# Twelve load slots for the small experts, and four accumulators for the last scatter

## The chip, the cores and the metric

The kernel runs on one core of a Trainium2 chip. The metric is the device time of one execution in microseconds (us). Most executions of a kernel here agree within 0.3%. A core has a matmul engine (TensorE, PE in the rows; its weight loads are PEld), a vector engine (VectorE, DVE), an activation engine (ScalarE, ACT), GpSimd (POOL) and SyncE (SP), which here issues the loads. Sixteen DMA engines move data from the chip's memory (HBM) into the on-chip memory (SBUF); matmuls accumulate in PSUM.

## The reference

A two-layer backbone over 256 latent tokens and 256 context tokens, width 1024: attention of three kinds, then a dense SwiGLU in layer 0 and a top-2-of-8 mixture of experts in layer 1, then a last RMSNorm. All in float32. The part that the change touches is the mixture and the norm behind it:

```python
def swiglu(h, wg, wu, wd):
    return (jax.nn.silu(h @ wg) * (h @ wu)) @ wd

def moe_swiglu(h, w_router, wg, wu, wd):
    t = h.reshape(-1, shp[-1])
    logits = (t @ w_router).astype(jnp.float32)
    top_v, top_i = lax.top_k(logits, TOP_K)
    top_w = jax.nn.softmax(top_v, axis=-1)
    gates = jnp.sum(jax.nn.one_hot(top_i, N_EXPERTS, dtype=jnp.float32) * top_w[..., None], axis=1)
    for e in range(N_EXPERTS):
        y = y + gates[:, e:e + 1].astype(t.dtype) * swiglu(t, wg[e], wu[e], wd[e])
...
        x = x + ga2[:, None] * ffn(h_lat)
...
    return rmsnorm(x, g_final)
```

Each expert has three matrices of 1024 x 3584 (wg, wu) and 3584 x 1024 (wd), 44 MB in float32, and all eight are read.

## The kernel before

The kernel works through layer 0, the attention of layer 1 and then, from about 1080 us on, the experts. Expert 0 comes first, the others in the order of how many tokens chose them. The first four (NBIG) get a block of 128 gathered tokens each and are called full here; the last four get 64 tokens and are called small.

A full expert (`expert`, L1184) reads weight blocks of 1 MB with `load_e` (L1076). Each block is converted on chip to a pair of float32r tiles, eh and el (`convert`, L788: ScalarE at L804, VectorE at L805), and TensorE multiplies with the pair in three passes (`mm3`). The converted tiles have buffers of their own: two of each kind in the pool `mpr` and one of each in `mpc`; loads take them in the order `(mpr, mpr, mpc)[i % 3]` (L1079), so the last two loads of the last full expert, number 174 and 175, have the two of `mpr`.

A small expert (`expert_small`, L1235) has half the rows and multiplies the loaded float32 block directly, with no conversion (`load_raw`, L1226). It goes through the 3584 hidden columns in four rounds j of 896. In a round come four times a gate and an up load of 256 x 896 (0.92 MB each) and their matmuls into `pgs` (L1274), then SiLU and product (L1284, L1285); the transposes (L1246) and the down step of the round before (`down_s`, L1251) come in the round after, with three loads of 256 x 1024 (1.05 MB), one of 128 x 1024 (0.52 MB) and matmuls into `pds` (L1261). So a round has twelve loads and 11.0 MB. The last down step of an expert, and the scatter of its result into the tokens (`t1`, L1298), run inside the first round of the expert after it.

Every load takes the next name of a list, the ring (`slot32`, L1066), takes its buffer, and puts the name back at the end. The ring begins with ten names; five of them leave at given load numbers (`until`, L914), and from load 62 on there are five: w, c, r0, r1, r2, of 1 MB each. The buffer is free when the instruction that last read it is done: VectorE's conversion for a load of a full expert, TensorE's last matmul on it for one of a small expert. The loads stand in one order on SyncE's queue, and a load that waits holds up all behind it. Besides that each load waits for the landing of the one eight before it, since eight semaphores (DMAHW0 to 7 in the order) tell of landings in turn.

The scatter (L1313 to L1322) scales the expert's 64 rows (VectorE, into the tile shown as xT), spreads them over the 256 tokens with four matmuls, two column halves o for each token half t, into `py`, one of two PSUM banks of the pool `pmt`, and adds each to the tokens `xtk` on VectorE. After the last expert `square` (L1337) does, for each column half, ScalarE's sum of squares and VectorE's product with the norm's gain into `xg`; `finish` (L1343) adds the sums, takes the root and scales and stores the output.

Of the kernel before, what the change touches and what calls it, by code (L numbers as in the profile page):

```python
# [11 lines left out]
F32 = mybir.dt.float32  # L12
# [3 lines left out]
AF = mybir.ActivationFunctionType  # L16
ALU = mybir.AluOpType
# [3 lines left out]
P = 128  # L21
# [6 lines left out]
NE = 8  # L28
# [4 lines left out]
NBIG = 4  # L33
# [58 lines left out]
def hybrid_backbone_kernel(  # L92
# [6 lines left out]
    act = nc.scalar.activation  # L99
    tt = nc.vector.tensor_tensor  # L100
# [33 lines left out]
    def bank(pool, name):  # L134
        return pool.tile([P, 512], F32, tag="b", name=name)
# [754 lines left out]
    for k in range(KD):  # L890
        t = tmp("nt2")[:, :NL]
# [4 lines left out]
    mp = pool("mp")  # L896
# [7 lines left out]

    slots = {"w": lambda: mpw.tile([P, 2048], F32, tag="w32", name="e32"),
             "c": lambda: mpc.tile([P, 2048], F32, tag="w32", name="e32"),
             "xh": lambda: mp.tile([P, 2048], F32, tag="xeH0", name="e32"),
             "xl": lambda: mp.tile([P, 2048], F32, tag="xeL0", name="e32"),
             "xt": lambda: mp2.tile([P, 2048], F32, tag="xtk", name="e32"),
# [85 lines left out]
    def part(ap, o):  # L995
        return ap[:, 2 * o:2 * o + 2]

    def half(ap):
        return ap.rearrange("p (a n) -> p a n", n=NL)
# [235 lines left out]
    def expert_small(xs, wg, wu, wd, e, tail, hooks, end=None):  # L1235
        H = P // 2
        xv = xs[:, :, (e - NBIG) * H:(e - NBIG + 1) * H]
        pd = [None]

        HB = FB // 2  # L1240
        NB = FE // FB

        def g_Ts(g):
            pt = bank(pmt, "pgt")
            for q in range(FK):
                nc.tensor.transpose(pt[:, q * H:(q + 1) * H], g[0:H, q * P:(q + 1) * P], ident[0:H, 0:H])  # L1246
            gt = mp2.tile([P, FK, H], F32, tag="gts", name="gts")
            copy_bal(gt, pt[:, 0:FK * H].rearrange("p (q n) -> p q n", n=H))
            return gt

        def down_s(gt, j):  # L1251
            if pd[0] is None:
                pd[0] = pdn.tile([P, 512], F32, tag=f"pd{e % 2}", name="pds")
            for q0 in range(0, FK, 2):
                kn = min(2, FK - q0)
                r0 = j * FB + q0 * P
                w = load_raw(wd[r0:r0 + kn * P, :].rearrange("(k p) n -> p k n", p=P), kn, D)
                for k in range(kn):
                    q = q0 + k
                    for o in range(2):  # L1260
                        mm(pd[0][H * o:H * o + H, :], lhsT=gt[:, q, :], rhs=w[:, k, o * 512:(o + 1) * 512],  # L1261
                           start=j == 0 and q == 0, stop=j == NB - 1 and q == FK - 1, skip_group_check=True)

        prev = None
        for j in range(NB):
            ps = pgu.tile([P, 2, 512], F32, tag=("pg", "pu")[j % 2], name="pgs")
            for c in range(KD // 2):
                ws = [load_raw(w_ap[c * 256:(c + 1) * 256, j * FB:(j + 1) * FB].rearrange("(k p) n -> p k n", p=P), 2, FB)
                      for w_ap in (wg, wu)]
                for k in range(2):  # L1270
                    kk = 2 * c + k
                    for b in range(2):
                        for o in range(2):
                            mm(ps[H * o:H * o + H, b, 0:HB], lhsT=xv[:, kk, :], rhs=ws[o][:, k, b * HB:(b + 1) * HB],  # L1274
                               start=kk == 0, stop=kk == KD - 1, skip_group_check=True)
                if c == 1:
                    if prev is not None:
                        gt = g_Ts(prev)
                    elif tail:
                        tail[0]()  # L1280
            g = mp2.tile([P, FB], F32, tag="es", name="es")
            for b in range(2):
                gv = g[0:H, b * HB:(b + 1) * HB]
                act(gv, ps[0:H, b, 0:HB], AF.Silu)  # L1284
                tt(gv, gv, ps[H:P, b, 0:HB], ALU.mult)  # L1285
            if prev is not None:
                down_s(gt, j - 1)
            elif tail:
                tail[1]()
            prev = g  # L1290
            for f in (hooks or {}).get(j, ()):
                f()
        last = []

        def t0():
            last.append(g_Ts(prev))

        def t1():  # L1298
            if end:
                tc.keep_in_program_order(nc.scalar.preload_act_table_set(LN_EXP))  # L1300
                new_xg()
            down_s(last[0], NB - 1)
            pt = bank(pmt, "pst")
            for t in range(2):
                nc.tensor.transpose(pt[:, t * P:(t + 1) * P], f32(S[:, t, e, :]), ident)
            for t in range(2):
                mm(pt[:, 256:257], lhsT=f32(S[:, t, e, :]), rhs=gatp[:, t, e:e + 1], start=t == 0, stop=t == 1)
            ST = mp2.tile([P, 256], F32, tag="ST", name="STs", bufs=2)
            nc.vector.tensor_copy(ST, pt[:, 0:256])
            gs = mp.tile([P, 1], F32, tag="gs", name="gs", bufs=2)  # L1310
            nc.vector.tensor_copy(gs, pt[:, 256:257])
            yo = part(y32, e % 2)
            stt(yo, half(pd[0]), gs, ga2s, op0=ALU.mult, op1=ALU.mult)  # L1313
            for t in range(2):
                pys = []
                for o in range(2):
                    py = bank(pmt, "py")
                    mm(py, lhsT=ST[H * o:H * o + H, t * P:(t + 1) * P], rhs=yo[H * o:H * o + H], start=True, stop=True)
                    pys.append(py)
                for o in range(2):  # L1320
                    cs = slice(o * 512, (o + 1) * 512)
                    tt(xtk[:, t, cs], xtk[:, t, cs], pys[o], ALU.add)  # L1322
            if end:
                for o in range(2):
                    end(o)
        return t0, t1

    xg = None
# [5 lines left out]
    ssq4 = mp.tile([P, 2, 2], F32, name="ssq4")  # L1334
    junk = xT[:, 4:6, 0:NL]

    def square(o):  # L1337
        for t in range(2):
            xo = half(xtk[:, t, o * 512:(o + 1) * 512])
            act(junk, xo, AF.Square, accum_out=ssq4[:, t, o:o + 1])  # L1340
            tt(half(xg[:, t, o * 512:(o + 1) * 512]), xo, part(gfb, o), ALU.mult)

    def finish():  # L1343
        tt(ssq, ssq4[:, :, 0], ssq4[:, :, 1], ALU.add)
# [15 lines left out]
    xes = {}  # L1360
# [21 lines left out]
    for e in range(NE):  # L1382
        if e == 0:
            ws = [w[0, 0] for w in (wm_g, wm_u, wm_d)]
        else:
            ws = [w[0, ds(which[e], 1)].rearrange("o a b -> (o a) b") for w in (wm_g, wm_u, wm_d)]
        hooks = {j: f for (ee, j), f in plan.items() if ee == e}
        if e >= NBIG:
            tail = expert_small(xes[NBIG], *ws, e, tail, hooks, square if e == NE - 1 else None)
            continue  # L1390
        xe, h = (x01, e * P) if e < 2 else (xes[2], (e - 2) * P)
        xv = (xe[0][:, :, h:h + P], xe[1][:, :, h:h + P])
        gt_ = gates if e == 0 else gatp
        tail = expert(xv, *ws, lambda t, e=e: S[:, t, e, :], lambda t, e=e, g=gt_: g[:, t, e:e + 1], tail, hooks, e == 0)
    tail[0]()
    tail[1]()
    finish()

    cv = nc.values_load(cnti[0:1, 0:1], min_val=0, max_val=NL)
    with tc.If(cv > 0):  # L1400
        pc = mp3.tile([P, 2], F32, name="pc")
        gc = mp3.tile([P, 2], F32, name="gc")
        bc = mp3.tile([P, 1], F32, name="bc")
        S2 = mp3.tile([P, 2, P], F32R, name="S2")
        xe2 = xe_tiles(1)
        for blk in range(2):
            with tc.For_i(0, NE, 1) as ei:
                nc.vector.tensor_copy(pc, posm[:, :, ds(ei, 1)].rearrange("p t o -> p (t o)"))
                nc.vector.tensor_copy(gc, gates[:, :, ds(ei, 1)].rearrange("p t o -> p (t o)"))
                nc.vector.tensor_copy(bc, base[:, ds(ei, 1)])  # L1410
                ts_(pc, pc, bc, float(P * blk), op0=ALU.subtract, op1=ALU.subtract)
                for t in range(2):
                    ts_(S2[:, t, :], tb("iota", tab2, TAB_C), pc[:, t:t + 1], None, op0=ALU.is_equal)
                gather(lambda t: S2[:, t, :], P, xe2)
                xv = (xe2[0][:, :, 0:P], xe2[1][:, :, 0:P])
                sq_ = lambda w: w[0, ds(ei, 1)].rearrange("o a b -> (o a) b")
                for f in expert(xv, sq_(wm_g), sq_(wm_u), sq_(wm_d), lambda t: S2[:, t, :], lambda t: gc[:, t:t + 1], None):
                    f()
        new_xg()
        for o in range(2):  # L1420
            square(o)
        finish()


# [29 lines left out]
```

## Time and profile before

| | |
|---|---|
| median of 3 runs | 1977.64 us (1975.27 to 1979.37) |
| profiled execution | 1976.52 us, of it 1974.7 us between the first and the last instruction (the span) |
| TensorE busy in the span | 1816.8 us (92%) |
| VectorE, ScalarE busy | 979.2 us, 758.7 us |
| read from HBM | 477.39 MB |

Times in rows are microseconds from the span's start, unless marked ns. The share of the DMA engines is the time that packets took over sixteen engines' time; it can be a little over 1 where packets overlap. A wait in the rows is put down to what ended it. The small experts run from about 1500 us to the end.

### The profile page before, as it was taken

The numbers are of one execution on the slowest core, as the hardware profiler recorded it, in microseconds if no ns is written. First come the engines' busy times: TensorE is split into PE (matmuls) and PEld (weight loads), VectorE is DVE, ScalarE is ACT, GpSimd is POOL, SyncE is SP. The second block draws the span as 40 slices with busy tenths as digits, with TensorE's granted clock in tenths as the row PEclk, the third lists the DMA queues.
The fourth block names the chain that finished last, engine by engine and source line by source line (L and its number), as shares of the span: only waits on it lengthen the run. The fifth ranks groups of instructions, "written<-read, shape, count | busy, mean of one in ns | idle before, by whom it ended". The sixth has DMA issues, their size and how long they took to land.

```text
span 1974.7 us, 23529 instructions
## 1 busy us (share of the span) xinstructions
PE 1816.8 (92%) x9280; PEld 1259.1 (64%) x9280; DVE 979.2 (50%) x1294; ACT 758.7 (38%) x965; POOL 46.7 (2%) x75
## 2 busy tenths in 40 slices
PE   7998999999999999999899999999998878887876
PEld 4756766778877887777687878888785322222222
DVE  5474555633333345755678888988984101010101
ACT  3424454422222224345566777777662000000001
POOL 1030000000000000210000000000000000000000
PEclk8999999999999999999989999999999999999998
DMA  8765243342334334553489789999998999999996
GB/s 281 223 178 143 70 132 100 115 144 70 101 99 156 110 108 155 158 140 128 146 298 360 255 305 330 334 356 361 353 340 317 366 388 388 388 382 402 396 397 249
DMA packets 261922, 480.05 MB, mean 243 GB/s; under 512 B 11630, under 2 KB 141996, under 8 KB 261804
## 3 DMA queue, kind: packets, MB, share of 16 engines
q1 hardware_dynamic: 259296, 474.19, 67.8%
q0 software_dynamic: 1312, 2.62, 0.9%
q10 hardware_dynamic: 1196, 1.66, 0.3%
q8 instruction: 75, 1.23, 0.3%
q14 instruction: 43, 0.35, 0.1%
HBM read 477.39 MB, written 1.05 MB: 242 GB/s over the span
## 4 chain that ended last, share of the span: by engine, by line
PE 74%; DMA 15%; DVE 7%; ACT 3%; issue 2%; SPq 0%; POOL 0%; DVEq 0%; ACTq 0%; POOLq 0%
DMA e<-in_w_moe_up_dram 10%; PE pd L1146 8%; PE pgs L1274 6%; DMA e<-in_w_moe_down_dram 3%; PE pu L152 3%; PE pg L151 3%; PE pu L153 3%; PE pg L152 3%; PE pu L151 3%; PE pg L153 2%; PE pds L1261 2%; PE psg L151 2%; PE psu L151 2%; PE psu L152 2%; PE psu L153 2%; PE psd L151 2%
## 5 line engine op out<-in xcount | busy, mean ns | idle before, releaser
L805 DVE TENSOR_TENSOR el<-e,eh 128x2048 fp32r<-128x2048 f32 (+1 forms) x173 | 375.4, 2189 | 49.5 <-ACT eh L804 48.8
L804 ACT ACTIVATE eh<-e 128x2048 fp32r<-128x2048 f32 (+1 forms) x173 | 316.7, 1839 | 93.1 <-PE pu L153 32.7
L1274 PE MATMUL pgs<-e,xs 128*64 128x448 f32 x1024 | 228.7, 557 | 71.1 <-DMA e<-in_w_moe_up_dram 64.4
L1274 PEld LDWEIGHTS pgs<-e,xs 128*64 128x64 f32 x1024 | 75.6, 138 | 218.7 <-DMA e<-in_w_moe_up_dram 105.0
L144 ACT ACTIVATE wh<-w 128x2048 fp32r<-128x2048 f32 (+2 forms) x70 | 125.4, 1791 | 208.4 <-issue 80.0
L145 DVE TENSOR_TENSOR wl<-w,wh 128x2048 fp32r<-128x2048 f32 (+2 forms) x70 | 149.6, 2138 | 97.9 <-ACT wh L144 97.9
L1285 DVE TENSOR_TENSOR es<-es,pgs 64x448 f32<-64x448 f32 x32 | 19.9, 623 | 324.0 <-ACT es L1284 324.0
L1284 ACT ACTIVATE es<-pgs 64x448 f32<-64x448 f32 x32 | 17.2, 537 | 325.6 <-PE pgs L1274 315.2
L1261 PE MATMUL pds<-e,gts 128*64 128x512 f32 x448 | 109.6, 599 | 9.9 <-DMA e<-in_w_moe_down_dram 9.0
L151 PE MATMUL pg<-eh,xeH 128*128 128x512 f32 x224 | 89.7, 400 | 0.6 <-ACT eh L804 0.6
L151 PE MATMUL psp<-hH,wh 128*128 128x512 f32 (+1 forms) x224 | 86.7, 391 | 3.1 <-ACT hH L276 3.0
L152 PE MATMUL pg<-el,xeH 128*128 128x512 f32 x224 | 89.4, 399 | 0.0
L151 PE MATMUL pu<-eh,xeH 128*128 128x512 f32 x224 | 88.8, 397 | 0.0
L152 PE MATMUL pu<-el,xeH 128*128 128x512 f32 x224 | 88.2, 394 | 0.7 <-DVE el L805 0.6
L151 PE MATMUL psq<-wh,hH 128*128 128x256 f32 x304 | 88.5, 291 | 0.0
L153 PE MATMUL pg<-eh,xeL 128*128 128x512 f32 x224 | 88.5, 395 | 0.0
L152 PE MATMUL psq<-wl,hH 128*128 128x256 f32 x304 | 87.7, 289 | 0.0
L153 PE MATMUL pu<-eh,xeL 128*128 128x512 f32 x224 | 87.7, 391 | 0.0
L153 PE MATMUL psq<-wh,hL 128*128 128x256 f32 x304 | 87.4, 287 | 0.0
L152 PE MATMUL psp<-hL,wh 128*128 128x512 f32 (+1 forms) x224 | 86.1, 384 | 0.0
L153 PE MATMUL psp<-hH,wl 128*128 128x512 f32 (+1 forms) x224 | 85.6, 383 | 0.0
L1261 PEld LDWEIGHTS pds<-e,gts 128*64 128x64 f32 x448 | 32.0, 136 | 68.6 <-issue 39.0
(504 smaller groups left out, 3470.8 us busy)
## 6 DMA issues: line engine op xcount, KB each, us to landing
e<-in_w_moe_down_dram SPq DMA_DIRECT2D x103, 1024.0 KB, 7.9
e<-in_w_moe_gate_dram SPq DMA_DIRECT2D x64, 896.0 KB, 7.8
e<-in_w_moe_up_dram SPq DMA_DIRECT2D x64, 896.0 KB, 7.1
e<-in_w_moe_gate_dram SPq DMA_DIRECT2D x55, 1024.0 KB, 7.3
e<-in_w_moe_up_dram SPq DMA_DIRECT2D x55, 1024.0 KB, 6.5
wmod<-in_w_mod_dram SPq DMA_DIRECT2D x96, 512.0 KB, 5.7
w<-in_w_in_dram SPq DMA_DIRECT2D x24, 1024.0 KB, 8.0
w<-in_w_ffn_gate_dram SPq DMA_DIRECT2D x11, 1024.0 KB, 5.8
```

Source lines behind the costliest of these rows:

```text
L144: act(wh[:, :m], w32[:, :m], AF.Copy)
L145: tt(wl[:, :m], w32[:, :m], f32(wh[:, :m]), ALU.subtract)
L151: mm(ps, lhsT=sh, rhs=mh, start=first, stop=False)
L152: mm(ps, lhsT=sh, rhs=ml, start=False, stop=False)
L153: mm(ps, lhsT=sl, rhs=mh, start=False, stop=last)
L804: act(h3[:, b], w[:, b], AF.Copy)
L805: tt(l3[:, b], w[:, b], f32(h3[:, b]), ALU.subtract)
L1146: mm(pds[o], lhsT=gt[sh][:, q, :], rhs=w[mh][:, k, o * 512:(o + 1) * 512], start=a and j == 0 and q == 0, stop=z and j == NJ - 1 and q == 3)
L1261: mm(pd[0][H * o:H * o + H, :], lhsT=gt[:, q, :], rhs=w[:, k, o * 512:(o + 1) * 512], start=j == 0 and q == 0, stop=j == NB - 1 and q == F ...
L1274: mm(ps[H * o:H * o + H, b, 0:HB], lhsT=xv[:, kk, :], rhs=ws[o][:, k, b * HB:(b + 1) * HB], start=kk == 0, stop=kk == KD - 1, skip_group_c ...
L1284: act(gv, ps[0:H, b, 0:HB], AF.Silu)
L1285: tt(gv, gv, ps[H:P, b, 0:HB], ALU.mult)
```

## The change

The ring gets seven names more when the first small expert begins its second round: the two pairs of `mpr` (mh, ml, twice), the pair of `mpc` (ch, cl) and a tile of the first gather (xm). These were in use by the full experts alone. Names at the front are used first, so the first five loads of that round have the old slots, and the sixth is the first with a new one. The names are taken off again ahead of the branch for experts with too many tokens, which does not run on these inputs.

The last scatter writes its four results into the two double banks of the gate and up accumulators, which are free by then, in place of two banks in turn; its four additions are kept in order, and squares and products follow them all.

```diff
     slots = {"w": lambda: mpw.tile([P, 2048], F32, tag="w32", name="e32"),
              "c": lambda: mpc.tile([P, 2048], F32, tag="w32", name="e32"),
+             "mh": lambda: mpr.tile([P, 2048], F32, tag="wh", name="e32"),
+             "ml": lambda: mpr.tile([P, 2048], F32, tag="wl", name="e32"),
+             "ch": lambda: mpc.tile([P, 2048], F32, tag="wh", name="e32"),
+             "cl": lambda: mpc.tile([P, 2048], F32, tag="wl", name="e32"),
+             "xm": lambda: mp.tile([P, 2048], F32, tag="xeL1", name="e32"),
...
         for j in range(NB):
+            if e == NBIG and j == 1:
+                ring.extend(["mh", "ml", "mh", "ml", "ch", "cl", "xm"])
...
+            keep = tc.keep_in_program_order if end else lambda i: i
+            pys = {}
+            if end:
+                spare = [pgu.tile([P, 2, 512], F32, tag=tag, name="py") for tag in ("pg", "pu")]
             for t in range(2):
-                pys = []
                 for o in range(2):
-                    py = bank(pmt, "py")
+                    py = spare[o][:, t] if end else bank(pmt, "py")
                     mm(py, lhsT=ST[H * o:H * o + H, t * P:(t + 1) * P], rhs=yo[H * o:H * o + H], start=True, stop=True)
-                    pys.append(py)
+                    pys[t, o] = py
                 for o in range(2):
                     cs = slice(o * 512, (o + 1) * 512)
-                    tt(xtk[:, t, cs], xtk[:, t, cs], pys[o], ALU.add)
+                    keep(tt(xtk[:, t, cs], xtk[:, t, cs], pys[t, o], ALU.add))
             if end:
-                for o in range(2):
-                    end(o)
+                end()
...
-    def square(o):
+    def squares():
         for t in range(2):
-            xo = half(xtk[:, t, o * 512:(o + 1) * 512])
-            act(junk, xo, AF.Square, accum_out=ssq4[:, t, o:o + 1])
-            tt(half(xg[:, t, o * 512:(o + 1) * 512]), xo, part(gfb, o), ALU.mult)
+            for o in range(2):
+                act(junk, half(xtk[:, t, o * 512:(o + 1) * 512]), AF.Square, accum_out=ssq4[:, t, o:o + 1])
+        for t in range(2):
+            for o in range(2):
+                cs = slice(o * 512, (o + 1) * 512)
+                tc.keep_in_program_order(tt(half(xg[:, t, cs]), half(xtk[:, t, cs]), part(gfb, o), ALU.mult))
...
+    ring[:] = [nm for nm in ring if nm in ("w", "c", "r0", "r1", "r2")]
```

The order of SyncE's loads is the same before and after; what they wait for is not. The rows are the loads of the second round of the first small expert, from its fifth on, and the first of the third round, before the change (other instructions of the queue stand between them). PE_49 is a wait for TensorE, DVE_49 for VectorE, DMAHW0_49 to DMAHW7_49 one for the load eight back.

```order
L1232 DMA e32_11841<-in_w_moe_gate_dram 128x2x896 [waits DMAHW4_49,DVE_49]
L1232 DMA e32_11843<-in_w_moe_up_dram 128x2x896 [waits DMAHW5_49,PE_49]
L1232 DMA e32_11853<-in_w_moe_gate_dram 128x2x896 [waits DMAHW6_49,PE_49]
L1232 DMA e32_11855<-in_w_moe_up_dram 128x2x896 [waits DMAHW7_49,PE_49]
L1232 DMA e32_11871<-in_w_moe_down_dram 128x2x1024 [waits DMAHW0_49,PE_49]
L1232 DMA e32_11877<-in_w_moe_down_dram 128x2x1024 [waits DMAHW1_49,PE_49]
L1232 DMA e32_11883<-in_w_moe_down_dram 128x2x1024 [waits DMAHW2_49,PE_49]
L1232 DMA e32_11889<-in_w_moe_down_dram 128x1024 [waits DMAHW3_49,PE_49]
L1232 DMA e32_11894<-in_w_moe_gate_dram 128x2x896 [waits DMAHW4_49,PE_49]
```

The same loads after the change:

```order
L1237 DMA e32_11841<-in_w_moe_gate_dram 128x2x896 [waits DMAHW4_49,DVE_49]
L1237 DMA e32_11843<-in_w_moe_up_dram 128x2x896 [waits DMASW4_49,DMASW3_49,DMASW5_49,DMASW2_49,DMASW6_49,DMASW1_49,DMASW7_49,DMASW0_49,PE_49]
L1237 DMA e32_11853<-in_w_moe_gate_dram 128x2x896
L1237 DMA e32_11855<-in_w_moe_up_dram 128x2x896 [waits PE_49]
L1237 DMA e32_11871<-in_w_moe_down_dram 128x2x1024 [waits DMAHW5_49]
L1237 DMA e32_11877<-in_w_moe_down_dram 128x2x1024 [waits DMAHW6_49]
L1237 DMA e32_11883<-in_w_moe_down_dram 128x2x1024 [waits DMAHW7_49]
L1237 DMA e32_11889<-in_w_moe_down_dram 128x1024 [waits DMAHW0_49]
L1237 DMA e32_11894<-in_w_moe_gate_dram 128x2x896 [waits DMAHW1_49,PE_49]
```

Before, e32_11843 waits for TensorE's last matmul on e32_11807, the first load of its own round. After, it waits for the last full expert's matmuls on eh_11739, the converted load 174, and e32_11855 for those on eh_11757, load 175; the four down loads have no wait for TensorE, and e32_11894, the thirteenth load of the longer ring, is the one that waits for the matmuls on e32_11807. The DMASW names are loads of GpSimd that landed in layer 1's attention.

On VectorE the end of the program stood like this before, from the last scaling (xT) to the scaling of the output:

```order
L1313 SCALAR_TENSOR_TENSOR xT<-pds,gs,xT 128x2x256
L1322 TENSOR_TENSOR xtk<-xtk,py 128x512
L1341 TENSOR_TENSOR xg<-xtk,xT 128x512
L1322 TENSOR_TENSOR xtk<-xtk,py 128x512 x2
L1341 TENSOR_TENSOR xg<-xtk,xT 128x512
L1322 TENSOR_TENSOR xtk<-xtk,py 128x512
L1341 TENSOR_TENSOR xg<-xtk,xT 128x512 x2
L1344 TENSOR_TENSOR ssq<-ssq_7907 128x2
L1354 TENSOR_SCALAR xg<-xg,ssq 128x512 x2
```

It stands like this after:

```order
L1320 SCALAR_TENSOR_TENSOR xT<-pds,gs,xT 128x2x256
L1332 TENSOR_TENSOR xtk<-xtk,py 128x512 x4
L1353 TENSOR_TENSOR xg<-xtk,xT 128x512 x4
L1356 TENSOR_TENSOR ssq<-ssq_7907 128x2
L1366 TENSOR_SCALAR xg<-xg,ssq 128x512 x2
```

The four additions (xtk) are now ahead of the four products (xg); the sum of the squares (ssq) is behind all eight in both. TensorE's order is the same in both.

## Rows read from the trace of the kernel before

**Rows 1.** The chain that ended last, by line, from 1540 to 1956 us.
```profile
by line: DMA e<-in_w_moe_up_dram 44.4%; PE pgs L1274 23.7%; DMA e<-in_w_moe_down_dram 15.9%; PE pds L1261 9.2%; PE py L1318 2.1%; DVE es L1285 1.2%; ACT es L1284 1.1%; PE pgt L1246 0.7%; issue 0.7%; DVE xT L1313 0.5%; PE pbc L1063 0.5%; DVE
```
**Rows 2.** Busy times by stretch; the first row names the columns.
```profile
core 0: us, PE busy (x) PEld busy (x) DVE busy (x) ACT busy (x) POOL busy (x), PEclk, DMA share, GB/s
1525.00:1540.00 15.00, 15.00 (x64) 6.58 (x65) 5.33 (x8) 1.80 (x3) 0.00 (x0) 1.00 0.49 176
1690.00:1720.00 30.00, 24.94 (x111) 9.45 (x111) 1.59 (x4) 1.62 (x3) 0.00 (x0) 0.89 0.99 380
1765.00:1825.00 60.00, 45.11 (x214) 15.38 (x214) 3.12 (x5) 2.69 (x5) 0.00 (x0) 1.00 1.03 406
1810.00:1840.00 30.00, 22.79 (x113) 8.35 (x113) 2.36 (x5) 1.07 (x2) 0.00 (x0) 1.00 1.02 400
1540.00:1955.00 415.00, 327.99 (x1530) 114.96 (x1526) 36.29 (x62) 21.81 (x39) 0.00 (x0) 0.99 1.01 391
```
**Rows 3.** TensorE's waits, 1540 to 1955 us: us in total, times, longest us.
```profile
PE pgs L1274 <- DMA e<-in_w_moe_up_dram: 61.7, 48, 2.7
PE pds L1261 <- DMA e<-in_w_moe_down_dram: 8.4, 15, 2.2
PE pgs L1274 <- DMA e<-in_w_moe_gate_dram: 5.2, 8, 0.8
```
**Rows 4.** Waits of SyncE's queue, 1509 to 1540 us.
```profile
SPq L1232 <- PE pgs L1274: 17.7, 3, 10.0
```
**Rows 5.** Waits of SyncE's queue, 1540 to 1956 us.
```profile
SPq L1232 <- PE pgs L1274: 212.2, 74, 7.2
SPq L1232 <- PE pds L1261: 82.2, 59, 3.3
```
**Rows 6.** SyncE's queue in order of time: start us, us.
```profile
1522.64 0.37 SPq L1232 DMA_DIRECT2D e<-in_w_moe_gate_dram  x1
1533.24 0.37 SPq L1232 DMA_DIRECT2D e<-in_w_moe_up_dram  x1
```
**Rows 7.** DMA, 1525 to 1537 us, in 40 slices of 0.3 us.
```profile
DMA  9999960000000000000000000000001971799999
GB/s 418 418 430 406 406 251 24 36 24 0 0 0 0 0 0 0 0 0 0 0 0 0 0 0 0 0 0 0 0 0 48 191 96 72 299 394 442 418 449 394
```
**Rows 8.** TensorE in order of time, 1517 to 1529 us: start us, us.
```profile
1523.51 1.04 PE L1146 MATMUL pd<-eh,gtl 128*128 128x512 f32 x2
...
1527.81 0.63 PE L1146 MATMUL pd<-eh,gtl 128*128 128x512 f32 x2
```
**Rows 9.** DMA, 1527 to 1956 us: packets, MB, share; then issues, KB each, us to landing.
```profile
q1 hardware_dynamic: 46635, 164.23, 98.7%
q8 instruction: 13, 0.21, 0.2%
q14 instruction: 6, 0.05, 0.0%
...
e<-in_w_moe_gate_dram SPq DMA_DIRECT2D x57, 896.0 KB, 7.9
```
**Rows 10.** DMA, 1948 to 1960 us, in 40 slices of 0.3 us.
```profile
GB/s 396 451 369 382 410 410 410 396 410 423 382 410 410 423 437 410 410 396 396 396 410 369 300 232 205 150 109 68 0 0 0 0 0 0 0 0 0 0 0 0
```
**Rows 11.** VectorE in order of time, 1956 to 1968 us: start us, us.
```profile
1960.59 0.69 DVE L1322 TENSOR_TENSOR xtk<-xtk,py 128x512 f32<-128x512 f32 x1 [1.22 <-PE py L1318]
...
1964.42 1.28 DVE L1341 TENSOR_TENSOR xg<-xtk,xT 128x512 f32<-128x512 f32 x2
1965.62 0.15 DVE L1344 TENSOR_TENSOR ssq<-ssq 128x2 f32<-128x2 f32 x1
```
**Rows 12.** ScalarE in order of time, 1960 to 1968 us: start us, us.
```profile
1965.33 0.18 ACT L1340 ACTIVATION_READ_ACCUMULATOR xT<-xtk 128x1 f32 x1
```
**Rows 13.** TensorE's weight loads, waits from 1540 to 1956 us.
```profile
PEld pgs L1274 <- issue: 80.8, 327, 0.8
PEld pds L1261 <- issue: 38.2, 135, 1.3
```

More of the change, by code (lines that the diff above doesn't have):

```diff
@@ L1388, in hybrid_backbone_kernel @@
         if e >= NBIG:
-            tail = expert_small(xes[NBIG], *ws, e, tail, hooks, square if e == NE - 1 else None)
+            tail = expert_small(xes[NBIG], *ws, e, tail, hooks, squares if e == NE - 1 else None)
             continue
@@ L1419, in hybrid_backbone_kernel @@
         new_xg()
-        for o in range(2):
-            square(o)
+        squares()
         finish()
```

## The prediction

> **What bounds the kernel now.** I read the chain that ended last first, for the stretch of the small experts (1540 to 1956 us): weight loads make 60% of it, 44.4% gate and up loads and 15.9% down loads, TensorE's small matmuls 33% [rows 1]. Then the busy times by stretch: from 1540 to 1955 us the DMA engines are filled (share 1.01) at 391 GB/s, while TensorE is busy 328 of 415 us [rows 2]. So the stage is a stream of weights. TensorE waits 75 us in it for landings (61.7 + 8.4 + 5.2) [rows 3], and has 87 us to spare.
>
> Then I asked whether the stream runs at what it can. It does not: between 1765 and 1825 us it holds 406 GB/s for 60 us, in other 30 us it falls to 380 and, right at the start of the stage (1525 to 1540 us), to 176 with a share of 0.49 [rows 2]. What holds it back is seen on SyncE's queue: its next load waits for TensorE to release a slot, 17.7 us in three waits at the start, the longest 10.0 us [rows 4], and 212 + 82 us in 133 waits after that [rows 5]. Those waits are harmless while older loads are still in flight, and cost where the queue runs dry. The reader is to see one hole in full: the load issued at 1522.64 us is followed by the next only at 1533.24 us [rows 6]; the rate is 251 GB/s in the slice that begins at 1526.5 us, nothing at all moves from 1527.7 us, and it is back at 394 GB/s from 1535.5 us [rows 7].
>
> **The ring, part by part.** The loads, their order and their bytes are unchanged; only what each waits for is. Load 6 after the extension (e32_11843) waited for the first load of its own round (five slots back), which TensorE could use only after finishing the last full expert. Now it takes the older of the two converted buffers that this expert's last down step read. TensorE's last matmul pair on it starts at 1523.51 us and takes 1.04 [rows 8], so the release is at 1524.6 us, not at 1533.2. The next load waits for nothing, the one after for the second buffer, whose last pair starts at 1527.81 and takes 0.63 us: 1528.4 us [rows 8]. Four down loads follow with no wait on TensorE at all. The first wait on a consumer in the new order is that of load 13, for the same release at 1533.2 us that load 6 had; by then seven loads, 6.42 MB or 15.8 us at 406 GB/s, have been queued. The hole is closed.
>
> From 1527 us to the end of the stage 164.23 MB come through queue q1 [rows 9]; by sizes that is all loads from number 6 on (57 gate, 58 up, 64 down). Before, they end in a taper, 300 GB/s in the slice at 1954.6 us to 68 in the one at 1956.1, that is at 1956.4 us [rows 10]. The taper costs 1.0 us against a full rate (0.3 us x (6 x 406 - 1064) / 406) and I keep it.
>
> With no hole, the 164.23 MB start where the earlier loads end, 1526.8 us. What is their rate? The trace gives two ends. Highest for a sustained stretch: 406 (the 60 us row), 404.5 us. Lowest: 391, today's mean with all its dips, 420.0 us. A stretch with an expert switch in it and few dips is at 400 (1810 to 1840 us) [rows 2], 410.6 us. I take 403, between 406 and 400, since deeper slots should remove the dips, while the switches themselves I can't exclude: 407.5 us. The end is 1526.8 + 407.5 + 1.0 = 1935.3 us, 21.1 us ahead of 1956.4. About 8 us of it is the hole, 13 us the dips.
>
> Twelve slots aren't twelve loads in flight: each load also waits for the landing of the one eight before it, by the eight DMA semaphores in the order. Eight loads are some 7.3 MB, 18 us of stream; the longest gap that the ring of five showed was 10.0 us [rows 4], so eight cover it. TensorE does not become the limit: its 328 us of work [rows 2] stand against 407 us of stream. It enters some 13 us of loads behind, and gains about 5 us per 27 us of loads (11.0 MB at 403 GB/s, 79% busy), so it has caught up within 70 us, and the end is again landing, last down step, tail. Slots cost no conversion and no copy; they were free since the full experts' last reads.
>
> A page of the Trainium skill speaks against this: "DMA: Bandwidth & Descriptors", section "Where 436 GB/s comes from", holds that loads from HBM are bound by a share of about 358 GB/s per core. By that figure the 164.23 MB would need 459 us, no depth would help, and the saving would be nothing. The trace disagrees: it already moves 391 GB/s over 415 us and 406 over 60 [rows 2].
>
> **The tail, part by part.** Four PSUM accumulators replace two, so that the second token half's matmuls no longer wait for VectorE's additions, and VectorE's eight operations stand as four additions, then four products. Before, VectorE has no idle time there: from the first addition at 1960.59 to the sum of squares at 1965.62 us eight operations run in 5.03 us, 0.63 each, pairs without a wait in 1.28 [rows 11]. The eight stay, and the sum still stands behind them. Bounds: eight at 0.60, the pitch in such a pair (1.28 less the 0.69 of one single is 0.59, rounded up), make 4.8, eight at 0.69 make 5.5; so -0.2 to +0.5 us. I take -0.1, as dependent neighbours are now further apart. ScalarE's squares, which ended 0.1 us before the sum (1965.33 + 0.18) [rows 12], get their inputs earlier and end ahead of VectorE's products; that wait goes, and the products are what is late. TensorE's second pair ends about as the second addition does.
>
> **Sum.** 21.1 + 0.1 = 21.2 us off the profiled execution, 1976.52 us (span 1974.7): 1955.3 us. The median of the runs, 1977.64, is 1.1 above it, so 1956.
>
> **Rivals.**
> 1. Only the hole goes; the dips are the memory's own, whatever the depth. For it: the DMA share stays at 0.99 to 1.00 where the rate is 380 [rows 2], so engines look filled. Against: TensorE's release holds back 133 loads [rows 5], and in the stretch with share 1.03 the rate is 406. Time: at 391 GB/s 420.0 us, end 1947.8, saving 8.6: 1969.
> 2. The stream gets faster than any long stretch shows, as single slices of 0.3 us are (418 GB/s at 1525.0 and 1525.3 us [rows 7]). 392.9 us, end 1920.7, saving 35.7: 1942. Against: 60 us in a row give 406. The Trainium skill's "HBM Reference", "Specifications (TRN2)", has about 425 for a core alone; an estimate from that figure is 386 us of stream, end 1914. No stretch here holds it.
> 3. It does not deliver: another wait ends last, for instance TensorE's or the landings of eight loads back. Then 1977. Against: its 87 us to spare, and landings are no wait while the stream runs.
> 4. Slower, by code. Instructions come over the same 16 engines: 13 fetches on q8 and 6 on q14 in this stage [rows 9]. If a fetch has to stand behind the loads queued, eight of them in place of at most five put each fetch up to three loads, 3 x 0.92 MB / 406 = 6.8 us, later. If each of 19 ended in a stall of TensorE, which is then what is late, that is 129 us, less 21: 2085; with the 13 of q8 alone 88 less 21: 2044. It decides from 21.2 / 19 = 1.1 us of stall per fetch. Against: with up to five loads queued today no wait of TensorE's weight loads without a visible releaser, where a late fetch would stand, is longer than 0.8 us at the gate and up lines and 1.3 at the down line [rows 13].
>
> **How the numbers follow.** Forecast 0.76: 1956, its own range 1950 to 1963 (406 gives 1976.52 - 24.2 + 1.1 = 1953.4, 400 gives 1959.5; two or three us more on each side for the spread of the runs, 1975.27 to 1979.37, and for the tail). Rival 1 0.10, rival 2 0.04, rival 3 0.05, rival 4 0.05. The range for 8 in 10: 1946 to 1967; it takes in what lies between the forecast and the first two rivals and leaves out their ends. What 0.2% can tell is 4 us: slower is rival 4, 0.05; the same is most of rival 3, 0.04; faster 0.91.
>
> **What would show it.** No hole at 1527 to 1535 us: the DMA share there at 1.0. From 1540 us to the stage's end 400 to 407 GB/s in every 30 us. SyncE's waits for TensorE in the stage gone or turned into waits for landings, the time to landing of a gate load from 7.9 us [rows 9] to 14 or more. TensorE's granted clock near 1.00, the 2.4 GHz level, as it was over the stage (0.99) [rows 2]. The last landing about 21 us earlier, and the time from it to the end the same within 0.5 us. Wrong it is if the rate stays near 391 with the queue never dry (rival 1), or if TensorE shows idle time that no landing ends (rival 4).

## The result and the profile after

| | kernel before | changed kernel |
|---|---|---|
| median of its runs, us | 1978.5 | 1957.6 |
| profiled execution, us (span) | 1976.52 (1974.7) | 1956.98 (1955.2) |
| first small weight load issued, us | 1483.49 | 1485.79 |
| from there to the end of the span, us | 491.2 | 469.4 |
| rate in 1525–1540 us, GB/s | 176 | 393 |
| rate over 300 us of the stage (1600–1900 us), GB/s | 392 | 407 |
| a gate load, issue to landing, us | 7.9 | 17.3 |

The ratio is 0.9893 with a 95% interval of 0.9864 to 0.9922, so 21 us (15 to 27) off 1978.5; the forecast was 1956 us, 21.2 us off the profiled execution. One execution of the changed kernel took 5055 us and stands outside the ratio; none of the 45 later ones of kernels with a longer ring did that, and its cause was not looked into.

The chain that ended last, by line, from 1540 to 1936 us, against [rows 1]:

```profile
by line: DMA e<-in_w_moe_up_dram 55.9%; DMA e<-in_w_moe_down_dram 23.3%; PE pgs L1281 9.4%; PE pds L1266 5.7%; ACT es L1291 1.7%; DVE es L1292 1.6%; PE py L1328 0.7%; issue 0.6%; PE pgt L1251 0.4%; DVE xT L1320 0.4%; SPq L1237 0.3%; DVE xtk
```

Weight loads are 79% of it, where they were 60%. TensorE's small matmuls, 33% before, are 15%: the chain hardly passes any more through a slot that TensorE has to release first.

Busy times by stretch, with the columns of [rows 2]:

```profile
1500.00:1525.00 25.00, 18.75 (x86) 8.70 (x85) 6.74 (x7) 5.16 (x5) 0.00 (x0) 0.90 0.88 333
1525.00:1540.00 15.00, 15.00 (x56) 6.84 (x55) 5.33 (x8) 1.26 (x2) 0.00 (x0) 0.94 1.02 393
1540.00:1570.00 30.00, 28.22 (x146) 10.53 (x146) 2.23 (x4) 2.15 (x4) 0.00 (x0) 1.00 1.03 407
1690.00:1720.00 30.00, 23.18 (x115) 8.38 (x113) 2.36 (x5) 1.07 (x2) 0.00 (x0) 1.00 1.03 407
1810.00:1840.00 30.00, 23.72 (x117) 8.79 (x118) 2.36 (x5) 1.07 (x2) 0.00 (x0) 1.00 1.03 407
1600.00:1900.00 300.00, 241.73 (x1135) 83.37 (x1136) 28.89 (x49) 14.54 (x27) 0.00 (x0) 0.99 1.03 407
```

The hole has gone (0.49 to 1.02 of share), and so have the dips: the stretch that stood at 380 GB/s and the one with an expert switch that stood at 400 are at 407, as 300 us in a row are. TensorE's work is the same; it is the queue that no longer runs dry. What a dip was shows in the kernel before, in SyncE's queue (start us, us) and DMA in slices of 0.3 us from 1702 us on:

```profile
1695.15 0.37 SPq L1232 DMA_DIRECT2D e<-in_w_moe_gate_dram  x1
1702.16 0.37 SPq L1232 DMA_DIRECT2D e<-in_w_moe_up_dram  x1
```

```profile
GB/s 430 358 251 191 203 131 167 215 370 370 406 461 394 370 394 442 370 406 430 406 454 382 370 418 406 442 418 406 428 413 420 433 393 394 423 396 423 178 109 123
```

No load was issued for 7.0 us, 6.4 of them a wait for TensorE's `pgs` matmuls; that is about the time that one took to land (7.9 for a gate load); the rate fell to 131 GB/s, and it was back at 370 from 1704.4 us on, after the next load had gone out. SyncE's queue of the changed kernel at the hole, in order of time (start us, us), against [rows 6]:

```profile
1524.76 0.37 SPq L1237 DMA_DIRECT2D e<-in_w_moe_gate_dram  x1
1526.72 0.37 SPq L1237 DMA_DIRECT2D e<-in_w_moe_up_dram  x1
1527.30 0.37 SPq L1237 DMA_DIRECT2D e<-in_w_moe_gate_dram  x1
1530.64 0.37 SPq L1237 DMA_DIRECT2D e<-in_w_moe_up_dram  x1
1531.21 2.16 SPq L1237 DMA_DIRECT2D e<-in_w_moe_down_dram  x4
```

After the load at 1524.76 us the next comes 1.96 us later, in place of 10.6, and the four down loads go out together. From 1509 to 1540 us SyncE now waits for the down-step matmuls of the last full expert (`pd`), as the new order says (us in total, times, longest us):

```profile
SPq L1237 <- PE pd L1151: 3.9, 2, 2.8
```

It still waits for TensorE after that (1540 to 1936 us, against [rows 5]):

```profile
SPq L1237 <- PE pgs L1281: 93.8, 69, 3.1
SPq L1237 <- PE pds L1266: 51.7, 34, 2.9
SPq L1237 <- PE py L1328: 10.2, 6, 1.9
SPq L1237 <- DMA e<-in_w_moe_down_dram: 5.0, 7, 1.6
```

With three smaller rows of TensorE (9 us) that is 165 us where 294 were, and the longest is 3.1 us where it was 7.2. These are the harmless kind: the 17.3 us to landing, at 407 GB/s, are 7.0 MB, seven to eight loads of 0.92 MB under way while SyncE waits. TensorE's waits for landings fell from 75 us [rows 3] to 60, and its weight loads' waits without a visible releaser are what they were [rows 13]:

```profile
PE pgs L1281 <- DMA e<-in_w_moe_up_dram: 54.5, 45, 1.5
PE pgs L1281 <- DMA e<-in_w_moe_gate_dram: 2.9, 4, 1.0
PE pds L1266 <- DMA e<-in_w_moe_down_dram: 2.4, 6, 0.6
```

```profile
PEld pgs L1281 <- issue: 80.7, 334, 0.8
PEld pds L1266 <- issue: 41.3, 153, 0.7
```

What was lost is at the end. DMA from 1928.4 us in slices of 0.3 us, against [rows 10]:

```profile
GB/s 437 423 451 396 410 396 369 369 396 423 423 369 341 314 259 232 205 205 178 164 164 164 164 164 109 55 55 14 14 0 0 0 0 0 0 0 0 0 0 0
```

The stream now runs down over 17 slices instead of 6. Against a full rate that is 0.3 us x (17 x 407 - 2801) / 407 = 3.0 us, where it was 1.0. And in the tail (VectorE, then TensorE, in order of time: start us, us; in brackets the idle time before and what ended it), against [rows 11]:

```profile
1940.99 1.28 DVE L1332 TENSOR_TENSOR xtk<-xtk,py 128x512 f32<-128x512 f32 x2 [1.22 <-PE py L1328]
1942.90 1.28 DVE L1332 TENSOR_TENSOR xtk<-xtk,py 128x512 f32<-128x512 f32 x2 [0.62 <-PE py L1328]
1944.10 2.49 DVE L1353 TENSOR_TENSOR xg<-xtk,xT 128x512 f32<-128x512 f32 x4
1946.51 0.16 DVE L1356 TENSOR_TENSOR ssq<-ssq 128x2 f32<-128x2 f32 x1
```

```profile
1939.83 1.13 PE L1328 MATMUL py<-xT,STs 64*128 64x512 f32 x4 [0.85 <-DVE xT L1320]
1941.74 1.72 PE L1328 MATMUL py<-xT,STs 64*128 64x512 f32 x4 [0.78 <-DVE xtk L1332]
```

In the kernel before, TensorE's second pair stood like this:

```profile
1961.33 1.12 PE L1318 MATMUL py<-xT,STs 64*128 64x512 f32 x2 [0.77 <-DVE xtk L1322]
```

From the first addition to the sum of squares it is 5.52 us, where it was 5.03: TensorE's second pair still waits 0.78 us for VectorE's additions, and VectorE, whose additions now stand together, has no product to do meanwhile and idles 0.62 us.

### The profile page after: what moved, and what is told of

The parts are those of the page before. It is cut to its first block, busy times and chain, and to the rows that moved or that the text cites. A ratio compares the mean times of both kernels' runs of the same rounds, so it can differ in the third digit from the quotient of the medians.

```text
span 1955.2 us, 23530 instructions
## 1 busy us (share of the span) xinstructions
PE 1811.9 (93%) x9280; PEld 1259.2 (64%) x9280; DVE 979.4 (50%) x1294; ACT 758.9 (39%) x965; POOL 46.6 (2%) x75
## 4 chain that ended last, share of the span: by engine, by line
PE 70%; DMA 18%; DVE 7%; ACT 3%; issue 2%; SPq 0%; POOL 0%; DVEq 0%; ACTq 0%; POOLq 0%
DMA e<-in_w_moe_up_dram 12%; PE pd L1151 8%; DMA e<-in_w_moe_down_dram 5%; PE pgs L1281 3%; PE pu L152 3%; PE pg L151 3%; PE pu L153 3%; PE pg L152 3%; PE pu L151 3%; PE pg L153 3%; PE psg L151 2%; PE psg L152 2%; PE psg L153 2%; PE psmod L231 2%; PE psu L151 2%; PE psu L152 2%
## 5 line engine op out<-in xcount | busy, mean ns | idle before, releaser
L1281 PE MATMUL pgs<-e,xs 128*64 128x448 f32 x1024 | 223.4, 550 | 61.4 <-DMA e<-in_w_moe_up_dram 57.1
L1291 ACT ACTIVATE es<-pgs 64x448 f32<-64x448 f32 x32 | 17.2, 537 | 306.4 <-PE pgs L1281 296.1
L1151 PE MATMUL pd<-eh,gth 128*128 128x512 f32 x224 | 71.2, 400 | 2.6 <-ACT eh L804 2.4
## 6 DMA issues: line engine op xcount, KB each, us to landing
e<-in_w_moe_gate_dram SPq DMA_DIRECT2D x64, 896.0 KB, 17.3
```

Source lines behind the costliest of these rows:

```text
L1151: mm(pds[o], lhsT=gt[sh][:, q, :], rhs=w[mh][:, k, o * 512:(o + 1) * 512], start=a and j == 0 and q == 0, stop=z and j == NJ - 1 and q == 3)
```

## The experiments

My theory: two gains that add up, a hole at the start that slots close on their first use, and dips that disappear because more loads are queued for the whole stage; the new tail gives nothing. The rivals: the gain is all of one kind (hole or depth); or the tail has part of it; or twelve slots matter, not eight in flight.

**1. The ring alone, with the tail of before.** The changed kernel's slots, ring and trim in the kernel before (the slots' definitions are left out below); the scatter, squares and products as they were.

```diff
 in before.py:
+            if e == NBIG and j == 1:
+                ring.extend(["mh", "ml", "mh", "ml", "ch", "cl", "xm"])
...
+    ring[:] = [nm for nm in ring if nm in ("w", "c", "r0", "r1", "r2")]
```

> The ring of twelve with the tail of the kernel before. Theory (the ring's slots give everything, the new tail costs about 0.5 us because TensorE's second pair still waits for VectorE): about 0.5 us under the changed kernel, ratio to before 0.988 to 0.990, 407 GB/s in the stage, VectorE 5.0 us from the first addition to the sum of squares. Rival (the tail has a share in the gain): 2 us or more over the changed kernel, ratio 0.991 or above.

Measured: 1957.56 us, ratio 0.9901 (0.9879 to 0.9923), 19.6 us, and 407 GB/s from 1600 to 1900 us: the whole gain, within the interval. On the tail it is not conclusive. The old tail took 5.99 us here, not 5.03, since TensorE's last matmuls ran at a mean granted clock of 0.70, so part of them at the lower level of 1.2 GHz, after it had waited for VectorE; the four `py` matmuls of the second group took 3.40 us against the 1.72 above. Busy times by stretch, then TensorE in order of time, of this kernel:

```profile
1942.00:1948.00 6.00, 4.52 (x8) 1.09 (x8) 3.94 (x7) 2.17 (x6) 0.00 (x0) 0.70 0.01 3
```

```profile
1943.90 3.40 PE L1325 MATMUL py<-xT,STs 64*128 64x512 f32 x4 [0.78 <-DVE xtk L1329]
```

**2. The tail alone.** The changed kernel with the ring left at five.

```diff
-            if e == NBIG and j == 1:
-                ring.extend(["mh", "ml", "mh", "ml", "ch", "cl", "xm"])
```

> The new tail with the ring of five. Theory: the time of before, at most 0.5 us more; VectorE's first addition to the sum of squares 5.5 us in place of 5.0, with an idle 0.6 us before the third addition that TensorE ends; the stage at 391 GB/s with the hole of 8 us at its start. Rival (the tail has a share in the gain): ratio under 0.998.

Measured: 1975.44 us, ratio 1.0005 (0.9988 to 1.0021). The tail is worth nothing that the time can tell; from the first addition to the sum it takes the same 5.52 us as in the changed kernel, with the same idle time of VectorE:

```profile
1958.09 1.28 DVE L1330 TENSOR_TENSOR xtk<-xtk,py 128x512 f32<-128x512 f32 x2 [0.62 <-PE py L1326]
```

**3. The added slots for one lap.** Each of the seven is taken once and not put back, so the hole may close while the rest of the stage runs on five.

```diff
-            ring.append(nm)
+            if nm not in ("mh", "ml", "ch", "cl", "xm"):
+                ring.append(nm)
```

> Twelve slots for one lap only: the seven new names are used once and not put back, then the ring is five again. Theory (8 us are the hole at the start, 13 the dips after it): the hole is gone and the dips stay, 385 to 393 GB/s from 1570 us on; 8 to 10 us saved, ratio 0.995 to 0.996. Rival (the dips are the memory's own or belong to the hole's after-effects, and the gain is all in the first lap): the time of the changed kernel, ratio 0.989, 405 GB/s or more throughout.

Measured: 1969.57 us, ratio 0.9963 (0.9949 to 0.9976), 7.3 us (4.7 to 10.1). Its stretches:

```profile
1525.00:1540.00 15.00, 15.00 (x56) 6.66 (x55) 5.44 (x9) 1.26 (x2) 0.00 (x0) 0.95 1.00 376
1600.00:1900.00 300.00, 237.38 (x1095) 81.67 (x1097) 28.35 (x48) 13.53 (x26) 0.00 (x0) 0.98 1.00 392
```

The hole is gone (376 for 176 GB/s) and the dips are all there (392). The time is the one that the forecast's first rival gave (1969 us), but the dips here come with a ring that is five again, not whatever the depth.

**4. The extension one round later.** The hole's loads go out before the slots are there; the dips' loads have them.

```diff
-            if e == NBIG and j == 1:
+            if e == NBIG and j == 2:
```

> The seven names join one round later, at the third round of the first small expert. Theory: the hole of 8 us at the stage's start stays, the dips go; 12 to 14 us saved, ratio 0.993 to 0.994, the stream stands still for 7 to 8 us near 1530 us and runs at 407 GB/s from 1570 us on. Rival (the gain is all in the first lap): no saving, ratio 0.998 or above.

Measured: 1963.88 us, ratio 0.9942 (0.9920 to 0.9964), 11.5 us (7.1 to 15.8). Stretches, then SyncE's queue:

```profile
1525.00:1540.00 15.00, 15.00 (x63) 6.25 (x63) 5.33 (x8) 1.80 (x3) 0.00 (x0) 1.00 0.52 185
1600.00:1900.00 300.00, 244.50 (x1131) 85.25 (x1129) 28.97 (x49) 14.54 (x27) 0.00 (x0) 0.98 1.03 407
```

```profile
1522.96 0.37 SPq L1237 DMA_DIRECT2D e<-in_w_moe_gate_dram  x1
1533.65 0.37 SPq L1237 DMA_DIRECT2D e<-in_w_moe_up_dram  x1
```

The mirror of the third: the hole of 10.7 us as before, and 407 GB/s after it. The two halves are 7.3 and 11.5 us, 18.8 together, against 19.6 for both in one kernel on the same chip (experiment 1); the intervals are wider than the difference. Two gains, and they add up.

**5. Eight slots in place of twelve.**

```diff
-                ring.extend(["mh", "ml", "mh", "ml", "ch", "cl", "xm"])
+                ring.extend(["mh", "ml", "mh"])
```

> Three new names in place of seven, so a ring of eight. Theory (eight DMA semaphores let no more than eight loads be in flight, and the waits of the ring of five were at most 10 us): within 3 us of the changed kernel, ratio 0.989 to 0.9915, 404 to 407 GB/s from 1570 us on. Rival (twelve are needed, since a slot is held by TensorE for long after its load has landed): 395 to 400 GB/s, ratio 0.993 to 0.995.

Measured: 1959.3 us, ratio 0.9926 (0.9897 to 0.9955). The ratio lies between what the theory and the rival had, and its interval takes in both; the rate decides. Its stretches and the start of its queue:

```profile
1525.00:1540.00 15.00, 15.00 (x63) 6.35 (x64) 5.33 (x8) 1.69 (x3) 0.00 (x0) 0.98 0.99 375
1540.00:1570.00 30.00, 27.43 (x139) 10.79 (x135) 2.49 (x4) 2.04 (x5) 0.00 (x0) 1.00 1.02 400
1600.00:1900.00 300.00, 239.41 (x1133) 83.22 (x1131) 28.39 (x47) 14.54 (x27) 0.00 (x0) 1.00 1.03 407
```

```profile
1529.19 0.37 SPq L1237 DMA_DIRECT2D e<-in_w_moe_up_dram  x1
1533.96 1.00 SPq L1237 DMA_DIRECT2D e<-in_w_moe_down_dram  x2
```

In the steady stage eight do what twelve do, 407 GB/s. At the start they don't: the down loads must wait for TensorE (a gap of 4.8 us). What that costs is not shown. The stage, from its first load to the end, takes 471.7 us in place of 469.4, but up to TensorE's last run of down-step matmuls it is 451.0 us against 450.4, and that time alone lies between 450.0 and 452.6 in kernels with the ring of the changed one (experiments 9 and 1). The rest, 1.7 us, is the tail, which the slots don't touch; 0.8 of it is VectorE's piece from the first addition to the sum (6.33 us), which waited for TensorE's second group of `py` matmuls, run at a mean granted clock of 0.66:

```profile
1941.19 2.54 PE L1328 MATMUL py<-xT,STs 64*128 64x512 f32 x4 [0.77 <-DVE xtk L1332]
```

The run down at the end costs about 2.3 us here. That is more than the 1.0 of five slots, but it can't be told from twelve: the same changed kernel, 3.0 above, loses 2.2 us in experiment 9. Its DMA from 1925.9 us on, in slices of 0.3 us:

```profile
GB/s 410 437 451 410 382 410 341 382 396 437 437 410 410 355 328 328 287 259 246 246 205 191 178 150 164 164 123 68 14 0 0 0 0 0 0 0 0 0 0 0
```

**6. Slots that are free earlier.** The changed kernel still has 333 GB/s in 1500 to 1525 us: its load of 1497.28 us is followed by one at 1503.42, waiting for TensorE. Three of the added slots (`ch`, `cl`, `xm`) were not in use by then, so this kernel gives them to the ring one round earlier.

```diff
+            if e == NBIG and j == 0:
+                ring.extend(["ch", "cl", "xm"])
             if e == NBIG and j == 1:
-                ring.extend(["mh", "ml", "mh", "ml", "ch", "cl", "xm"])
+                ring.extend(["mh", "ml", "mh", "ml"])
```

> The three names that no load of the last full expert uses any more (ch, cl, xm) join one round earlier, at the first small round; the four others as in the changed kernel. Theory (what is left of the stream's standing still, near 1502 us and between 1508 and 1530 us, is slots again): the gap near 1502 us goes, the last full expert's down step comes 3 to 6 us earlier, 3 to 6 us under the changed kernel, ratio 0.986 to 0.9875. Rival (there the conversions and TensorE's last full expert set the pace): within 1 us of the changed kernel, ratio 0.989.

Measured: 1950.35 us, ratio 0.9888 (0.9861 to 0.9914). By the ratio this is not to be told from the changed kernel (0.9893), as the rival had it. The trace does tell. Its stretch and its queue there:

```profile
1500.00:1525.00 25.00, 21.01 (x90) 10.62 (x84) 6.78 (x8) 5.16 (x5) 0.00 (x0) 0.86 1.03 408
```

```profile
1494.30 0.37 SPq L1237 DMA_DIRECT2D e<-in_w_moe_gate_dram  x1
1494.88 0.37 SPq L1237 DMA_DIRECT2D e<-in_w_moe_up_dram  x1
1495.46 0.37 SPq L1237 DMA_DIRECT2D e<-in_w_moe_gate_dram  x1
1496.03 0.94 SPq L1237 DMA_DIRECT2D e<-in_w_moe_up_dram  x1
```

The same mechanism at another place: the loads go out one behind the other, 333 GB/s become 408, and the stage takes 465.2 us, 4.2 less than in the changed kernel; all of it is gained ahead of TensorE's last run of down-step matmuls (446.2 us in place of 450.4).

**7. A tail without the wait.** The first token half's sums go to accumulators of their own, so that no tile is shared by the halves; half the products go into the last scaling.

```diff
-                    py = spare[o][:, t] if end else bank(pmt, "py")
+                    py = spare[o][:, 0] if end and t == 0 else bank(pmt, "py")
...
-            for o in range(2):
-                cs = slice(o * 512, (o + 1) * 512)
-                tc.keep_in_program_order(tt(half(xg[:, t, cs]), half(xtk[:, t, cs]), part(gfb, o), ALU.mult))
+            tc.keep_in_program_order(tt(half(xg[:, t, 0:512]), half(xtk[:, t, 0:512]), part(gfb, 0), ALU.mult))
...
-                    nc.vector.tensor_scalar_mul(xo, xo, ssq[:, t:t + 1])
+                    stt(half(xo), half(xtk[:, t, cs]), ssq[:, t:t + 1], part(gfb, o), op0=ALU.mult, op1=ALU.mult)
```

> The changed kernel with four separate accumulator tiles in the last scatter (two of the pool pmt, two of the spare ones), the sum of squares ahead of the second half's products, and these products fused with the last scaling on VectorE. Theory (TensorE's second pair waits because both halves of one tile are held together, not for want of a bank): VectorE's idle time before the third addition goes, four additions back to back in 2.5 us, and the sum of squares comes 3.7 to 4.3 us after the first addition in place of 5.5; 1 to 2 us saved. Rival (VectorE waits for TensorE's matmul time, whatever the tiles): the idle 0.6 us stays.

Measured: 1955.32 us, ratio 0.9900 (0.9873 to 0.9928): by the time alone not to be told from the changed kernel. The trace does tell. VectorE, then TensorE:

```profile
1944.39 2.48 DVE L1332 TENSOR_TENSOR xtk<-xtk,py 128x512 f32<-128x512 f32 x4 [1.22 <-PE py L1328]
1946.79 1.28 DVE L1351 TENSOR_TENSOR xg<-xtk,xT 128x512 f32<-128x512 f32 x2
1948.13 0.16 DVE L1354 TENSOR_TENSOR ssq<-ssq 128x2 f32<-128x2 f32 x1
```

```profile
1943.23 1.99 PE L1328 MATMUL py<-xT,STs 64*128 64x512 f32 x8 [0.85 <-DVE xT L1320]
```

All eight matmuls stand in one run with no wait between the halves, the four additions back to back in 2.48 us, and from the first addition to the sum it is 3.74 us where the changed kernel has 5.52. Of these 1.78 us the idle time is 0.62; most of the rest is the two products that moved, and they come back as 0.53 us in the last scaling (1.41 for 0.88), so about 1.25 us are left. From TensorE's last run of down-step matmuls to the end it is 17.2 us in place of 19.0. The stage as a whole was no shorter in this execution (469.8 us), as its start ran at 365 GB/s in place of 393.

**8. Both, 6 and 7.** The two edits above in one kernel.

> Both of the last two together. Theory: their savings add, 4 to 8 us under the changed kernel, ratio 0.985 to 0.987. If one of the two fails, what is left of the other.

Measured: 1949.28 us, ratio 0.9872 (0.9846 to 0.9897); the stage takes 462.2 us.

**9 and 10. The changed kernel and the eighth once more, side by side,** unchanged, in five rounds on one chip, to tell the two apart.

> The changed kernel as it is, beside the next on one chip. Theory: ratio 0.989 to 0.990 to the kernel before, as in its first timing.

> The early ring and the second tail together, again, now beside the changed kernel on one chip. Theory: 6 to 8 us under the changed kernel, ratio to before 0.985 to 0.987. Rival (its lead was the difference of two chips): within 2 us of the changed kernel.

Measured: the changed kernel 1955.68 us, ratio 0.9897 (0.9877 to 0.9917); the one with both edits 1947.9 us, ratio 0.9856 (0.9834 to 0.9878). It is 7.8 us below the changed kernel and the fastest version here. Its stage takes 462.0 us and that of the changed kernel 469.3; of these 7.3 us 5.0 lie ahead of TensorE's last run of down-step matmuls and 2.3 behind it, so the larger part is the slots given earlier.

**11. Five slots again at the end.** If the longer run down comes from more loads being under way, cutting the ring back for the last round should shorten it.

```diff
+            if e == NE - 1 and j == NB - 1:
+                ring[:] = [nm for nm in ring if nm in ("w", "c", "r0", "r1", "r2")]
```

> The changed kernel, but the seven names leave the ring ahead of the last round of the last expert. Theory (the stream ends in a longer taper than before because with eight loads in flight the DMA engines drift apart): the taper's loss goes from 2.9 us to about 1, while the last round's 20 loads run with five slots; together within 2 us of the changed kernel. Rival (the taper comes from the last loads' sizes, not from the depth): the taper stays at 2.5 to 3 us.

Measured: 1957.96 us, ratio 0.9909 (0.9883 to 0.9935). DMA from 1928.5 us in slices of 0.3 us, and the stretch ahead of it:

```profile
GB/s 369 369 396 382 423 396 423 423 437 423 396 382 382 423 410 423 437 423 369 410 382 423 355 150 55 27 27 27 0 0 0 0 0 0 0 0 0 0 0 0
```

```profile
1900.00:1930.00 30.00, 24.82 (x115) 8.80 (x111) 1.73 (x4) 2.90 (x4) 0.00 (x0) 0.94 0.97 379
```

The run down is short again (0.3 us x (6 x 407 - 641) / 407 = 1.3 us), so its length does follow the number of slots at the end. But the last round ran at 379 GB/s, which gives back what the end saved. No gain; why the run down is longer with more slots was not seen.

## Why the prediction was right

The first two steps held as they were put. **The hole closed** by the release that was named, the two converted buffers of the last full expert; the fourth experiment takes just that away and has the hole back, the third has just that and gains 7.3 us against the 8 forecast. **The dips went** because the queue was too short: with the same loads, bytes and order, five slots give 392 to 394 GB/s over 300 us (experiments 3 and 2), eight or twelve 407. It gained 11.5 us against 13. **That eight in flight are enough** held in the steady stage; at the start eight slots leave a gap of 4.8 us, whose cost was not measured.

Three terms were mis-sized, and partly cancel:
- The rate. 403 GB/s was taken, between 400 and 406, for fear of the expert switches. It is 407 in every long stretch, switches included: 403.5 us for the 164.23 MB, 4.0 better than forecast.
- The run down. Kept at 1.0 us, it is 3.0: 2.0 worse. That it depends on the slots was not thought of. Read in the same way it is 1.1 and 1.8 us with five slots at the end (experiments 2 and 3), 1.3 with twelve cut back to five (experiment 11), and 2.2 to 3.5 in the eight traces of kernels that keep twelve; so 3.0 is one value out of a spread.
- The start. 15 us at 393 rather than 407 GB/s are 0.5 us worse.

One step failed: **the tail.** It was to lose 0.1 us because "the second token half's matmuls no longer wait for VectorE's additions". They do wait, 0.78 us, as they had before (0.77): before for want of a free accumulator, now because both halves share one accumulator tile, and the second half's matmul waits for the reader of the first. With the products no longer between the additions VectorE idles 0.62 us, and the piece is 0.5 us longer, 0.6 off the forecast, at the upper bound that was given. The seventh experiment, with separate tiles, has neither the wait nor the idle time. In experiment 2 the total feels nothing of it that can be measured.

With the stage starting 2.3 us later in the profiled execution, with nothing changed ahead of it, the sum is 1955.3 - 4.0 + 2.0 + 0.5 + 0.6 + 2.3 = 1956.7 us; measured 1956.98. It leaves out what follows the sum of squares: scaling and store took 0.4 us less, so that from TensorE's last run of down-step matmuls to the end of the span it is 19.0 us for 18.9, although the piece on VectorE is 0.5 longer. With that the sum is 1956.3, so 0.7 us stay without a cause, and the agreement is partly luck.

One sign was read wrongly in advance: SyncE's waits for TensorE did not go or turn into waits for landings, they fell from 294 to 165 us, and those for landings make 10 us (6 before). The other signs came: the time to landing is 17.3 us ("14 or more"), the rate 406 to 407 GB/s in every 30 us from 1540 to 1930, the last landing, by TensorE's last run of down-step matmuls, 19.6 us earlier and 21.9 with the later start counted, and the time from there to the end 0.1 us longer.

Of the rivals, the first, dips whatever the depth, is excluded by the same 407 GB/s over 300 us with the longer ring, with the hole (experiment 4) or without it. The second, 418 GB/s, is excluded by 407 over 300 us. The third is excluded by the chain, 79% loads. The fourth began to count at 1.1 us of stall for each of 19 fetches; TensorE's weight loads have no longer waits without a visible releaser than before (0.8 and 0.7 us, 122 us in total for 119). On the page of the Trainium skill that spoke against the change, "DMA: Bandwidth & Descriptors", "Where 436 GB/s comes from": its share of about 358 GB/s does not bound these loads, which hold 407 for 300 us. The about 425 for a core alone of the Trainium skill's "HBM Reference", "Specifications (TRN2)", is not reached in any long stretch here.

## What to carry to other kernels

In a stage bound by loads, look at the rate in stretches of 15 to 30 us and not at the mean: where it falls below the best one that the same stage holds, see what the queue's next load waits for, and whether a buffer that is dead by then can take its place. Count when each such buffer becomes free, for a slot given one round too late costs as much as one that is missing (11.5 against 21 us here, and by the traces 4 to 5 more for three of the slots one round earlier). Accumulators are only as separate as the tiles they are in; check in the order who waits for whom before the wait is counted as gone.

## What the runs showed of the hardware

- More slots, longer run down: 1.0 to 1.8 us lost in three traces with five slots at the end and 1.3 with twelve cut back to five, but 2.3 with eight and 2.2 to 3.5 in eight traces with twelve. Eight and twelve are not told apart by this; either way at most eight loads are under way, by the landing that each load waits for.
- 407 GB/s is what the DMA engines held for 300 us on end, in every kernel with eight slots or more; with five it was 392 to 394.
- TensorE's granted clock fell in the tail of experiments 1, 3 and 5. Over the second group of `py` matmuls its mean was 0.58, 0.62 and 0.66, so part of the group ran at the lower level of 1.2 GHz, and the group took 3.40, 2.67 and 2.54 us for the 1.72 of the changed kernel. Each time TensorE had just waited 0.77 or 0.78 us for VectorE; but it had waited as long in the changed kernel and in experiments 2, 4, 6, 9 and 11, whose second group took 1.72 us. What decides was not seen. It lengthens the piece from the first addition to the sum by 0.8 to 1.0 us, more than the edit of the tail moved it.
